# Row sums with a constant matrix as weights, and the norm's factor computed on 128x256

## The chip, the cores and the metric

The kernel runs on one core of one Trainium2 chip. Its time is the device time of one execution in microseconds; times within the trace count from the start of the profiled span. Engines: TensorE (PE, its weight loads PEld), VectorE (DVE), ScalarE (ACT), GpSimd (POOL) and SyncE (SP), which issues most DMAs.

## The reference, cut to what matters

Three transformer blocks run one after the other on a sequence of 256 tokens of width 1024. Block 1 is two mixers, a layer norm, an expert layer with product keys and a second layer norm. Block 2 is two layers of a mixer (nsa, then fox) and a squared-ReLU MLP, with a root-mean-square norm before and after each. Block 3 is mlstm, a gated feed-forward layer, hgrn and a mixture of experts, each behind a norm, and a final norm. What the change touches is the factor of these norms:

```python
def rms_norm(x, g):
    xf = x.astype(jnp.float32)
    y = xf * lax.rsqrt(jnp.mean(xf * xf, axis=-1, keepdims=True) + NORM_EPS)
    return (y * g.astype(jnp.float32)).astype(x.dtype)

def layer_norm(x, g, b):
    ...
    var = jnp.mean(jnp.square(xf - mu), axis=-1, keepdims=True)
    y = (xf - mu) * lax.rsqrt(var + LN_EPS) * g.astype(jnp.float32) + b.astype(jnp.float32)

# in the second block
x = x + rms_norm(m, norm_g[i, 1])
h = rms_norm(x, norm_g[i, 2])
x = x + rms_norm(squared_relu_mlp(h, mlp_w_up[i], mlp_w_down[i]), norm_g[i, 3])
```

## The kernel before

Activations lie transposed in SBUF: the 1024 features are eight tiles of 128 partitions (KT = 8), and the 256 tokens are the columns (T = 256). A norm therefore sums over partitions, which a matmul does, and its factor is one number per token, that is per column, and the same on all partitions.

Weights are streamed from HBM in tiles raw of 128x1024 by SyncE's queue. ScalarE rounds each into hi (L316) and VectorE forms the rest lo (L317), four buffers of each; mm3 (L327 to L329) makes three matmuls out of every product. lin_chunk makes one accumulator mm of 128x512 out of 48 such matmuls; there are two mm buffers.

A norm goes like this. Squares collects the squares of eight tiles of x in two tiles of 128x512: the first is the sum of three pairs, the second holds the last pair. fold (L494) sums each over partitions by add_sum (L359): the data are the weights, the constant column onesD is what moves, and the outcome is 128x2 in PSUM, tokens on partitions. It makes 8 matmul calls, each two passes in the trace. rstd (L371) computes the factor on 128x2: the root on ScalarE (L376), then v, the reciprocal, two products and a last step on VectorE (L377 to L381):

```python
nc.scalar.activation(t, var, AF.Sqrt, bias=self.C(eps))
nc.vector.tensor_scalar(v, var, eps, -0.5, op0=OP.add, op1=OP.mult)
nc.vector.reciprocal(r, t)
nc.vector.tensor_tensor(t, r, r, op=OP.mult)
nc.vector.tensor_tensor(t, t, v, op=OP.mult)
nc.vector.scalar_tensor_tensor(r, t, 1.5, r, op0=OP.add, op1=OP.mult)
```

spread (L388) brings the 128x2 back to 128x256 on all partitions by two matmul calls, four passes, into PSUM (L391):

```python
self.nc.tensor.matmul(ps[:, i * 128:i * 128 + 128], r[:, i:i + 1].to_broadcast([128, 128]),
                      self.C("ident"), start=True, stop=True)
```

Five places of the code use the factor, called at fourteen places of the program. The layer norms (yk, L453) and rms (yk, L415) and the final norm (L2001) read it from PSUM. add_normed (L473) copies it to SBUF first (rsb, L475) and multiplies (yk, L480), four times. inverse (L504) copies both forms, icol of 128x2 and irow of 128x256 (L507, L508), and is called in nsa, in both squared-ReLU MLPs and in fox, where the factor is multiplied into the outcome of a product and not into its input. In the MLP that is hr (L1039), the first reader of an up chunk's accumulator. A fifteenth norm, the router's, uses its factor as 128x2.

No order is written out by hand: a scheduler places the instructions of each engine in one row, by the dependences and its own estimates, so a change of the norm's code also moves what stands around it.

Of the kernel before, what the change touches and what calls it, by code (L numbers as in the profile page):

```python
# [16 lines left out]
AF = mybir.ActivationFunctionType  # L17
OP = mybir.AluOpType
# [4 lines left out]
T = 256  # L23
# [8 lines left out]
ADDS = 4  # L32
LNV = 8
EPS = (1e-6, 1e-5)
BASE = ("warm", "rs_v", "rs_r", "rs_t", "sqk", "yk", "sq2", "icol")

INV_FREQ = np.float32(10000.0) ** (-np.arange(0, 64, 2, dtype=np.float32) / np.float32(64))

# [178 lines left out]
class Core:  # L217
# [61 lines left out]
    def small(self, shape, dt=F32, tag="s", bufs=2):  # L279
        pool = self.base if tag in BASE else self.kept.get(tag, self.sm)  # L280
        return pool.tile([128] + list(shape), dt, tag=tag, bufs=bufs, name=self.name(tag))
# [114 lines left out]

        self.nc.tensor.matmul(ps, self.C("onesD"), x, start=first, stop=last)

    def rstd_rows(self, sums, eps):
        return self.spread(self.ms_ps()[:, :T], self.rstd(sums[:, :2], eps))  # L400

    def squares(self, x):
        s = Squares(self)
# [64 lines left out]
    def add_normed(self, x, src, gm, sq, g=None):  # L468

        nc = self.nc
        r = self.rstd_rows(self.fold(sq), 1e-6)  # L473
        rs = self.small([T], tag="rsb", bufs=1)
        nc.scalar.activation(rs, r, AF.Copy)  # L475
        nxt = Squares(self, None if g is not None else nc.vector)
        parts = (self.big([KT, T], F32R, nm="nhi"), self.big([KT, T], F32R, nm="nlo")) if g is not None else None
        for k in range(KT):
            m = self.small([T], tag="yk", bufs=3)
            nc.vector.scalar_tensor_tensor(m, src(k), gm[:, k:k + 1], rs, op0=OP.mult, op1=OP.mult)  # L480
            eng = nc.vector if k < ADDS else nc.gpsimd
            eng.tensor_tensor(x[:, k], x[:, k], m, op=OP.add)
            if g is not None:
                self.scaled(x, k, g, parts)
            if k % 2:
                nxt.add(x[:, k - 1:k + 1])
        return nxt, parts
# [5 lines left out]

    def fold(self, sq):  # L494

        ps = self.sums()
        n = len(sq.tiles)
        for i, t in enumerate(sq.tiles):
            for f in range(2):
                self.add_sum(ps, 0, t[:, f], i + f == 0, i == n - 1 and f == 1, square=False)  # L500
        return ps

    def inverse(self, sums, eps=1e-6):

        r = self.rstd(sums[:, :2], eps)
        col, row = self.small([2], tag="icol", bufs=1), self.small([T], tag="irow", bufs=1)
        self.nc.vector.tensor_copy(col, r)  # L507
        self.nc.scalar.activation(row, self.spread(self.ms_ps()[:, :T], r), AF.Copy)  # L508
        return col, row

    def accumulate(self, w, hid, ys, first, last, dts=range(8)):

# [519 lines left out]
def squared_relu(c, x, sq, hs, l, g=None):  # L1032
    nc, d = c.nc, c.d
    ps0, inv = [], []

    def evac(ps):
        r = c.small([2, T], tag="hr")
        row = inv[0][1][:, None, :].to_broadcast([128, 2, T])
        nc.vector.scalar_tensor_tensor(r, ps, 0.0, row, op0=OP.max, op1=OP.mult)  # L1039
        s = c.small([2, T], tag="hs")  # L1040
        nc.scalar.activation(s, r, AF.Square)
        h = (c.small([2, T], F32R, tag="hhi"), c.small([2, T], F32R, tag="hlo"))
        c.split(s, h[0], h[1])
        return h

    def hidden(j):
        ps = c.lin_chunk(d[f"up{l}"][j], hs)
        if j == 0:
            inv.append(c.inverse(c.fold(sq)))
        return evac(ps)  # L1050

    ys = c.long_sum(16, hidden, d[f"down{l}"])
    squares = Squares(c, nc.vector)
    for b in range(4):
        squares.add(ys[b])
    return c.add_normed(x, lambda k: ys[k // 2][:, k % 2], c.V(f"ng{l}3"), squares, g)
# [14 lines left out]
def small_tok(c, src, n, xs):  # L1071

    nc = c.nc
    w = c.wsplit(src, KT)
    ps = c.ms_ps()[:n, :T]
    for k in range(KT):
        c.mm3(ps, w[k], (xs[0][:, k], xs[1][:, k]), k == 0, k == KT - 1)
    zt = c.small([T], tag="zt", bufs=1)
    nc.scalar.activation(zt[:n], ps, AF.Copy)
    pt = c.ms_ps()[:, :2 * n].rearrange("p (a b) -> p a b", a=2)  # L1080
    for tt in range(2):
        nc.tensor.transpose(pt[:, tt], zt[:n, tt * 128:tt * 128 + 128], c.C("ident")[:n, :n])
    return pt
# [8 lines left out]
def nsa(c, x, sq, hs):  # L1092
    nc, d = c.nc, c.d
# [7 lines left out]
    kc, vc = kc[:, 0], kc[:, 1]  # L1101
    K2 = c.big([4, 2, T], nm="K2")
    ps = c.lin_chunk(d["nsa_in"][4], hs)
    col, row = c.inverse(c.fold(sq))
    rv = rp.rearrange("p (a t) -> p a t", a=4)
    nc.vector.tensor_tensor(rv, rv, row[:, None, :].to_broadcast([128, 4, T]), op=OP.mult)

# [116 lines left out]
    ps = small_tok(c, d["nsa_g"], 48, hs)  # L1224
# [3 lines left out]
    v = c.big([2, 2, T], nm="nv")  # L1228
    for br in range(2):
        ps = c.tok_chunk(d["nsa_in"][8 + br], hs)  # L1230
# [67 lines left out]
def fox(c, x, sq, hs):  # L1298
    nc, d = c.nc, c.d
    causal = c.C("causal")  # L1300
    k, v = c.big([KT, T], nm="fk"), c.big([2, D], nm="fv")
# [1 line left out]
    pad_heads(c, q)  # L1303
    bf = bcast_row(c, d["rows16"], 0, 16, "bf")
    ps0 = c.lin_chunk(d["fox_in"][0], hs)
    col, row = c.inverse(c.fold(sq))
    row = row[:, None, :].to_broadcast([128, 2, T])
    z, lf = c.small([2, 16], tag="fz", bufs=1), c.small([2, 16], tag="flf", bufs=1)
    ps = small_tok(c, d["fox_f"], 16, hs)
# [3 lines left out]
    ps = c.ms_ps()  # L1313
# [6 lines left out]
    for j in range(4):  # L1320
        ps = c.lin_chunk(d["fox_in"][j], hs) if j else ps0
# [4 lines left out]
    for j in range(4):  # L1326
        ps = c.tok_chunk(d["fox_in"][8 + j], hs)
# [59 lines left out]
def block2(c, x, sq, hs):  # L1387

    with c.phase("nsa", 8):
        sq, hs = nsa(c, x, sq, hs)  # L1390
    with c.phase("mlp0", 8):
        sq, hs = squared_relu(c, x, sq, hs, 0, c.V("ng10"))
    with c.phase("fox", 8):
        sq, hs = fox(c, x, sq, hs)
    with c.phase("mlp1", 8):
        return squared_relu(c, x, sq, hs, 1)[0]
# [368 lines left out]
class Router:  # L1765
# [34 lines left out]

    def finish(self, sq):
        c, nc = self.c, self.c.nc
        r = c.rstd(c.fold(sq)[:, :2], 1e-6)
        lt = c.small([T], tag="lt", bufs=1)
        nc.scalar.activation(lt[:8], self.lg, AF.Copy)
        pt = c.ac_ps()[:, :16].rearrange("p (a e) -> p a e", a=2)
        lg = c.small([2, 8], tag="lg", bufs=1)
        for tt in range(2):
            nc.tensor.transpose(pt[:, tt], lt[:8, tt * 128:tt * 128 + 128], c.C("ident")[:8, :8])
        for tt in range(2):  # L1810
            nc.vector.scalar_tensor_tensor(lg[:, tt], pt[:, tt], r[:, tt:tt + 1], self.bias, op0=OP.mult, op1=OP.add)
        found = places(c, lg)
        parts = (c.big([2, D], F32R, nm="xhi"), c.big([2, D], F32R, nm="xlo"))
        for tt in range(2):
            for a in range(0, D, 512):
                w = slice(a, a + 512)
                t = self.xt[:, tt, w]
                nc.vector.scalar_tensor_tensor(t, t, r[:, tt:tt + 1], self.row[:, w], op0=OP.mult, op1=OP.add)
                c.split(t, parts[0][:, tt, w], parts[1][:, tt, w])
        return parts, found  # L1820
# [216 lines left out]
```

## Time and profile before

| | |
|---|---|
| median of 3 runs | 2934.7 us |
| lowest and highest run | 2927.17, 2935.34 us |
| the profiled execution | 2925.78 us |
| its span | 2924.1 us |
| mean granted TensorE clock | 0.975 of full speed |
| TensorE matmul busy | 2818.6 us, 96% |
| VectorE busy | 2063.4 us, 71% |
| ScalarE busy | 1543.8 us, 53% |
| GpSimd busy | 156.8 us, 5% |

A timeline row gives the start in us, the length in us, engine, line, operation, what is written and read, and how many instructions are merged into it; brackets hold the idle time of the engine before it and what ended it.

### The profile page before, as it was taken

How to read it: one execution, taken by the hardware profiler on the slowest of the kernel's cores; microseconds unless marked ns; L12 is line 12 of the kernel's file. 1: busy time of each engine (PE TensorE's matmuls, PEld its weight loads, DVE VectorE, ACT ScalarE, POOL GpSimd, SP SyncE). 2: the span in 40 equal slices, each digit the busy share in tenths (PEclk: the TensorE clock that was granted, in tenths of full speed). 3: DMA queues.
4: the chain of work that ended last, by engine and by line, in shares of the span. 5: the costliest groups of instructions: out<-in, count | busy, mean ns of one | idle time of the engine just before them, and what ended most of it. 6: DMA issues, size and time to landing. Idle time of an engine off the chain costs nothing. (4 is left out here: it accounts for less than half of the span.)

```text
span 2924.1 us, 51291 instructions
## 1 busy us (share of the span) xinstructions
PE 2818.6 (96%) x20880; PEld 2666.6 (91%) x20880; DVE 2063.4 (71%) x3757; ACT 1543.8 (53%) x2196; POOL 156.8 (5%) x137
## 2 busy tenths in 40 slices
PE   8999999899999999999999999989999998999998
PEld 8998989899999999887999989989899997888886
DVE  6655979777777785667655565565655696899997
ACT  5454317544444444457444464445544645777775
POOL 0000000000000000210001000001000170000000
PEclk9999999999999999899999999989999999999998
DMA  7543346888888786341454415534255432789885
GB/s 277 209 155 136 134 144 231 288 302 297 299 302 298 283 300 230 123 176 47 145 185 146 173 59 188 182 108 159 102 188 188 141 129 87 295 331 336 324 331 211
DMA packets 118901, 602.23 MB, mean 206 GB/s; under 512 B 10752, under 2 KB 46080, under 8 KB 49664
## 3 DMA queue, kind: packets, MB, share of 16 engines
q1 hardware_dynamic: 78480, 557.96, 53.1%
q10 hardware_dynamic: 40176, 40.91, 4.4%
q8 instruction: 166, 2.72, 0.4%
q14 instruction: 79, 0.65, 0.1%
HBM read 579.43 MB, written 19.39 MB: 205 GB/s over the span
## 5 line engine op out<-in xcount | busy, mean ns | idle before, releaser
L317 DVE TENSOR_TENSOR lo<-raw,hi 128x1024 fp32r<-128x1024 f32 x915 | 1126.2, 1244 | 590.4 <-ACT hi L316 586.9
L316 ACT ACTIVATE hi<-raw 128x1024 fp32r<-128x1024 f32 x915 | 960.9, 1057 | 926.5 <-PE mm L328 507.5
L327 PE MATMUL mm<-nhi,hi 128*128 128x256 f32 x1312 | 378.6, 290 | 10.2 <-ACT nhi L491 6.8
L328 PE MATMUL mm<-nlo,hi 128*128 128x256 f32 x1312 | 378.9, 289 | 0.5 <-DVE nlo L492 0.5
L329 PE MATMUL mm<-nhi,lo 128*128 128x256 f32 x1312 | 376.7, 287 | 0.0
L329 PE MATMUL mm<-lhi,lo 128*128 128x256 f32 x1024 | 295.1, 288 | 7.7 <-DVE lo L317 7.7
L327 PE MATMUL mm<-lhi,hi 128*128 128x256 f32 x1024 | 294.9, 289 | 5.1 <-ACT r L933 2.8
L328 PE MATMUL mm<-llo,hi 128*128 128x256 f32 x1024 | 295.6, 289 | 0.0
L328 PE MATMUL ac<-r,hi 128*128 128x256 f32 x1024 | 288.2, 282 | 0.0
L329 PE MATMUL ac<-r,lo 128*128 128x256 f32 x1024 | 288.0, 281 | 0.0
L327 PE MATMUL ac<-r,hi 128*128 128x256 f32 x1024 | 287.7, 281 | 0.0
L327 PEld LDWEIGHTS mm<-nhi,hi 128*128 128x128 f32 x1312 | 257.5, 197 | 12.2 <-ACT nhi L491 7.5
L328 PEld LDWEIGHTS mm<-nlo,hi 128*128 128x128 f32 x1312 | 257.7, 197 | 2.5 <-DVE nlo L492 1.7
L329 PEld LDWEIGHTS mm<-nhi,lo 128*128 128x128 f32 x1312 | 257.7, 197 | 0.1
L329 PEld LDWEIGHTS mm<-lhi,lo 128*128 128x128 f32 x1024 | 201.0, 196 | 9.0 <-DVE lo L317 8.1
L327 PEld LDWEIGHTS mm<-lhi,hi 128*128 128x128 f32 x1024 | 201.2, 197 | 6.9 <-ACT r L933 3.0
L328 PEld LDWEIGHTS mm<-llo,hi 128*128 128x128 f32 x1024 | 200.9, 196 | 1.1 <-issue 0.7
L328 PE MATMUL ac<-hlo,hi 128*128 128x256 f32 x688 | 193.0, 281 | 0.0
L328 PEld LDWEIGHTS ac<-r,hi 128*128 128x128 f32 x1024 | 192.9, 188 | 0.0
L327 PE MATMUL ac<-hhi,hi 128*128 128x256 f32 x688 | 192.8, 280 | 0.0
L329 PEld LDWEIGHTS ac<-r,lo 128*128 128x128 f32 x1024 | 192.7, 188 | 0.0
L327 PEld LDWEIGHTS ac<-r,hi 128*128 128x128 f32 x1024 | 192.7, 188 | 0.0
(590 smaller groups left out, 6288.9 us busy)
## 6 DMA issues: line engine op xcount, KB each, us to landing
raw<-in_moe_gu SPq DMA_DIRECT2D x88, 1024.0 KB, 5.1
raw<-in_peer_u SPq DMA_DIRECT2D x64, 1024.0 KB, 5.0
raw<-in_peer_v SPq DMA_DIRECT2D x64, 1024.0 KB, 5.5
raw<-in_ada SPq DMA_DIRECT2D x48, 1024.0 KB, 7.2
raw<-in_moe_d SPq DMA_DIRECT2D x40, 1024.0 KB, 5.5
raw<-in_up SPq DMA_DIRECT2D x32, 1024.0 KB, 4.9
raw<-in_down SPq DMA_DIRECT2D x32, 1024.0 KB, 4.9
raw<-in_ffn_gu SPq DMA_DIRECT2D x22, 1024.0 KB, 4.9
```

The source lines that it names most:

```text
L316: nc.scalar.activation(hi, raw[:, a:a + m], AF.Copy)
L317: nc.vector.tensor_tensor(lo, raw[:, a:a + m], hi, op=OP.subtract)
L327: mm(ps, w[0], x[0], start=start, stop=False, **k)
L328: mm(ps, w[0], x[1], start=False, stop=False, **k)
L329: mm(ps, w[1], x[0], start=False, stop=stop, **k)
```

## The change

fold sums with the constant matrix onesD (128x128) as weights, and the squares move, 256 columns a call (rows_add, which the layer norm's mean used already): 4 calls instead of 8, and the outcome is 128x256 in PSUM, the same on all partitions. The factor is computed on this 128x256 by the same six steps and stands in SBUF at the end. The spread, the copy rsb and the copy irow are gone. Where tokens are needed on partitions (icol in nsa and fox), column takes two columns out of irow with two matmuls of one column and a VectorE copy. The router keeps the old way under the name fold_cols. The scratch memory for dynamic DMA is halved.

```diff
+    def rstd_rows(self, sums, eps, out=None):
+        nc = self.nc
+        v, r, t = (self.small([T], tag=g, bufs=1) for g in ("rr_v", "rr_r", "rr_t"))
+        m = sums[:, :T]
+        nc.scalar.activation(t, m, AF.Sqrt, bias=self.C(eps))
+        nc.vector.tensor_scalar(v, m, eps, -0.5, op0=OP.add, op1=OP.mult)
+        nc.vector.reciprocal(r, t)
+        nc.vector.tensor_tensor(t, r, r, op=OP.mult)
+        nc.vector.tensor_tensor(t, t, v, op=OP.mult)
+        out = r if out is None else out
+        nc.vector.scalar_tensor_tensor(out, t, 1.5, r, op0=OP.add, op1=OP.mult)
+        return out
...
-    def rstd_rows(self, sums, eps):
-        return self.spread(self.ms_ps()[:, :T], self.rstd(sums[:, :2], eps))
...
-        r = self.rstd_rows(self.fold(sq), 1e-6)
-        rs = self.small([T], tag="rsb", bufs=1)
-        nc.scalar.activation(rs, r, AF.Copy)
+        rs = self.rstd_rows(self.fold(sq), 1e-6)
...
     def fold(self, sq):
+        ps = self.ms_ps()
+        n = len(sq.tiles)
+        for i, t in enumerate(sq.tiles):
+            for f in range(2):
+                self.rows_add(ps[:, :T], t[:, f], i + f == 0, i == n - 1 and f == 1)
+        return ps
...
     def inverse(self, sums, eps=1e-6):
-        r = self.rstd(sums[:, :2], eps)
-        col, row = self.small([2], tag="icol", bufs=1), self.small([T], tag="irow", bufs=1)
-        self.nc.vector.tensor_copy(col, r)
-        self.nc.scalar.activation(row, self.spread(self.ms_ps()[:, :T], r), AF.Copy)
-        return col, row
+        return self.rstd_rows(sums, eps, out=self.small([T], tag="irow", bufs=1))
+
+    def column(self, row):
+        ps = self.ms_ps()[:, :2]
+        for i in range(2):
+            self.nc.tensor.matmul(ps[:, i:i + 1], row[:, i * 128:i * 128 + 128], self.C("ident")[:, :1], start=True, stop=True)
+        col = self.small([2], tag="icol", bufs=1)
+        self.nc.vector.tensor_copy(col, ps)
+        return col
...
-    col, row = c.inverse(c.fold(sq))
+    row = c.inverse(c.fold(sq))
+    col = c.column(row)
...
-        r = c.rstd(c.fold(sq)[:, :2], 1e-6)
+        r = c.rstd(c.fold_cols(sq)[:, :2], 1e-6)
...
-    nc = bacc.Bacc("TRN2", target_bir_lowering=False, num_devices=1, dynamic_dma_scratch_size=8192)
+    nc = bacc.Bacc("TRN2", target_bir_lowering=False, num_devices=1, dynamic_dma_scratch_size=4096)
```

The change also moves instructions. On VectorE, at the norm in front of hgrn, the row before is this (rs_ are the small tiles of the factor, ms the spread factor, yk the normed input):

```order
L377 TENSOR_SCALAR rs_v_24364<-ms_24354 128x2 [waits Activation_49]
L378 RECIPROCAL rs_r_24365<-rs_t_24366 128x2
L379 TENSOR_TENSOR rs_t_24366<-rs_r_24365 128x2 [waits DVE_49]
L380 TENSOR_TENSOR rs_t_24366<-rs_t_24366,rs_v_24364 128x2 [waits DVE_49]
L381 SCALAR_TENSOR_TENSOR rs_r_24365<-rs_t_24366,rs_r_24365 128x2 [waits DVE_49]
L317 TENSOR_TENSOR lo_24478<-raw_24471,hi_24477 128x1024 [waits Activation_49]
L415 SCALAR_TENSOR_TENSOR yk_24377<-x,mg_24352,ms_24363 128x256 [waits PE_49]
```

and now, with rr_ for the factor's tiles:

```order
L405 TENSOR_SCALAR rr_v_24265<-ms_24260 128x256 [waits Activation_49]
L406 RECIPROCAL rr_r_24266<-rr_t_24267 128x256
L317 TENSOR_TENSOR lo_24377<-raw_24370,hi_24376 128x1024 [waits Activation_49]
L407 TENSOR_TENSOR rr_t_24267<-rr_r_24266 128x256 [waits DVE_49]
L408 TENSOR_TENSOR rr_t_24267<-rr_t_24267,rr_v_24265 128x256 [waits DVE_49]
L410 SCALAR_TENSOR_TENSOR rr_r_24266<-rr_t_24267,rr_r_24266 128x256 [waits DVE_49]
L426 SCALAR_TENSOR_TENSOR yk_24276<-x,mg_24258,rr_r_24266 128x256 [waits DVE_49]
```

The split lo, which stood behind the last step and ahead of yk, has moved between the reciprocal and the first product.

On VectorE, in the first squared-ReLU MLP, the row before runs from the second norm's small steps to the first hr:

```order
L378 RECIPROCAL rs_r_14935<-rs_t_14936 128x2
L379 TENSOR_TENSOR rs_t_14936<-rs_r_14935 128x2 [waits DVE_49]
L380 TENSOR_TENSOR rs_t_14936<-rs_t_14936,rs_v_14934 128x2 [waits DVE_49]
L381 SCALAR_TENSOR_TENSOR rs_r_14935<-rs_t_14936,rs_r_14935 128x2 [waits DVE_49]
L507 COPY icol_14943<-rs_r_14935 128x2 [waits DVE_49]
L317 TENSOR_TENSOR lo_15032<-raw_15025,hi_15031 128x1024 [waits PE_49,Activation_49]
L1039 SCALAR_TENSOR_TENSOR hr_14950<-mm_14876,irow_14944 128x512 [waits Activation_49]
```

and now:

```order
L317 TENSOR_TENSOR lo_14994<-raw_14987,hi_14993 128x1024 [waits PE_49,Activation_49]
L405 TENSOR_SCALAR rr_v_14903<-ms_14897 128x256 [waits Activation_49]
L406 RECIPROCAL rr_r_14904<-rr_t_14905 128x256 [waits DVE_49]
L407 TENSOR_TENSOR rr_t_14905<-rr_r_14904 128x256 [waits DVE_49]
L317 TENSOR_TENSOR lo_15048<-raw_15045,hi_15047 128x1024 [waits DMAHW5_49,PE_49,Activation_49]
L408 TENSOR_TENSOR rr_t_14905<-rr_t_14905,rr_v_14903 128x256 [waits DVE_49]
L410 SCALAR_TENSOR_TENSOR irow_14902<-rr_t_14905,rr_r_14904 128x256 [waits DVE_49]
L1062 SCALAR_TENSOR_TENSOR hr_14912<-mm_14848,irow_14902 128x512 [waits DVE_49]
```

One split has moved ahead of v, and one stands between the two products. The second MLP has the same rows.

On TensorE, in fox, the spread stood between the last matmuls of the first chunk and the narrow projection of 16 columns:

```order
L327 MATMUL mm_17004<-nhi_16927,hi_17000 128x256
L328 MATMUL mm_17004<-nlo_16928,hi_17000 128x256
L329 MATMUL mm_17004<-nhi_16927,lo_17001 128x256
L391 MATMUL ms_17074<-cst,rs_r_17063 128x128 [waits DVE_49,PE_49]
L391 MATMUL ms_17074<-cst,rs_r_17063 128x128
L327 MATMUL ms_17086<-nhi_16927,hi_17082 16x256 [waits PE_49]
```

and now the column stands there, behind the second chunk:

```order
L327 MATMUL mm_17089<-nhi_16880,hi_17085 128x256
L328 MATMUL mm_17089<-nlo_16881,hi_17085 128x256
L329 MATMUL mm_17089<-nhi_16880,lo_17086 128x256
L529 MATMUL ms_17021<-cst,irow_17011 128x1 [waits DVE_49,PE_49]
L529 MATMUL ms_17021<-cst,irow_17011 128x1
L327 MATMUL ms_17034<-nhi_16880,hi_17030 16x256
```

What TensorE waits for there has changed from the 128x2 factor to irow.

## Rows read from the trace of the kernel before

**Rows 1.** The page's busy time by engine: us, share, instructions.

```profile
PE 2818.6 (96%) x20880; PEld 2666.6 (91%) x20880; DVE 2063.4 (71%) x3757; ACT 1543.8 (53%) x2196; POOL 156.8 (5%) x137
```

**Rows 2.** TensorE's waits: us in total, times, the longest.

```profile
PE ms L391 <- DVE rs_r L381: 13.3, 10, 2.2
```

**Rows 3.** Timeline of the first layer norm.

```profile
273.36 3.17 PE L368 MATMUL ms<-cst,sq 128*128 128x1 f32 x16 [3.98 <-DVE sq L565]
...
276.56 0.26 ACT L376 ACTIVATE rs_t<-ms,cst 128x2 f32<-128x2 f32 x1 [2.13 <-PE ms L368]
...
276.94 0.15 DVE L378 RECIPROCAL rs_r<-rs_t 128x2 f32<-128x2 f32 x1
...
277.52 0.16 DVE L381 SCALAR_TENSOR_TENSOR rs_r<-rs_t,rs_r 128x2 f32<-128x2 f32 x1
...
277.73 1.22 PE L391 MATMUL ms<-cst,rs_r 128*128 128x128 f32 x4 [1.21 <-DVE rs_r L381]
278.99 0.75 DVE L453 TENSOR_TENSOR yk<-x,ms 128x256 f32<-128x256 f32 x2 [1.32 <-PE ms L391]
```

**Rows 4.** Timeline, TensorE: a mean in layer norm two, a fold.

```profile
1195.82 3.62 PE L397 MATMUL ms<-x,cst 128*128 128x256 f32 x16
...
1929.70 2.00 PE L368 MATMUL ms<-cst,sq 128*128 128x1 f32 x16
```

**Rows 5.** VectorE by line and shape: count, busy us, mean ns of one.

```profile
L453 DVE TENSOR_TENSOR yk<-x,ms 128x256 f32<-128x256 f32 x16 | 6.0, 414 | 2.6 <-PE ms L391 2.6
...
L378 DVE RECIPROCAL rs_r<-rs_t 128x2 f32<-128x2 f32 x15 | 2.3, 155 | 0.0
...
L378 DVE RECIPROCAL rs_r<-rs_t 128x8 f32<-128x8 f32 x4 | 0.8, 194 | 0.0
...
L1193 DVE RECIPROCAL cst<-cst 128x16 f32<-128x16 f32 x2 | 0.5, 253 | 0.1
```

**Rows 6.** Timeline, add_normed after nsa.

```profile
1387.19 0.26 ACT L376 ACTIVATE rs_t<-ms,cst 128x2 f32<-128x2 f32 x1 [0.87 <-PE ms L368]
...
1389.10 0.38 ACT L475 ACTIVATE rsb<-ms 128x256 f32<-128x256 f32 x1 [1.66 <-PE ms L391]
1389.52 0.88 DVE L480 SCALAR_TENSOR_TENSOR yk<-mix,vecs,rsb 128x256 f32<-128x256 f32 x2 [1.22 <-ACT rsb L475]
```

**Rows 7.** Timeline, add_normed after fox.

```profile
1734.30 0.26 ACT L376 ACTIVATE rs_t<-ms,cst 128x2 f32<-128x2 f32 x1 [0.87 <-PE ms L368]
...
1737.14 0.88 DVE L480 SCALAR_TENSOR_TENSOR yk<-mix,vecs,rsb 128x256 f32<-128x256 f32 x2 [1.73 <-ACT rsb L475]
```

**Rows 8.** Timeline, add_normed at the end of the second MLP.

```profile
1931.85 1.23 DVE L317 TENSOR_TENSOR lo<-raw,hi 128x1024 fp32r<-128x1024 f32 x1 [0.27 <-ACT hi L316]
...
1932.99 0.15 DVE L377 TENSOR_SCALAR rs_v<-ms 128x2 f32<-128x2 f32 x1
...
1935.54 0.88 DVE L480 SCALAR_TENSOR_TENSOR yk<-ac,vecs,rsb 128x256 f32<-128x256 f32 x2 [1.73 <-ACT rsb L475]
```

**Rows 9.** Timeline, the norm in front of hgrn.

```profile
2288.38 0.26 ACT L376 ACTIVATE rs_t<-ms,cst 128x2 f32<-128x2 f32 x1 [3.27 <-PE ms L368]
...
2289.61 1.23 DVE L317 TENSOR_TENSOR lo<-raw,hi 128x1024 fp32r<-128x1024 f32 x1
...
2290.86 1.26 DVE L415 SCALAR_TENSOR_TENSOR yk<-x,mg,ms 128x256 f32<-128x256 f32 x3
```

**Rows 10.** Timeline, inverse in the first MLP.

```profile
1407.14 0.39 ACT L508 ACTIVATE irow<-ms 128x256 f32<-128x256 f32 x1
```

**Rows 11.** Timeline, the spread in nsa.

```profile
1226.97 0.60 PE L391 MATMUL ms<-cst,rs_r 128*128 128x128 f32 x4
```

**Rows 12.** Stretches: length, busy by engine, granted clock; full clock, then twelve low stretches.

```profile
286.00:290.00 4.00, 4.00 (x35) 4.00 (x34) 2.32 (x5) 1.93 (x3) 0.00 (x0) 1.00 0.00 0
...
273.80:284.10 10.30, 7.95 (x35) 7.39 (x35) 5.82 (x21) 3.77 (x10) 0.00 (x0) 0.50 0.00 1
...
sum 117.40, PE 78.36 PEld 72.73 DVE 70.53 ACT 42.45 POOL 20.18; mean PE 6.53 PEld 6.06 DVE 5.88 ACT 3.54 POOL 1.68
```

More of the change, by code (lines that the diff above doesn't have):

```diff
@@ L34 @@
 EPS = (1e-6, 1e-5)
-BASE = ("warm", "rs_v", "rs_r", "rs_t", "sqk", "yk", "sq2", "icol")
+BASE = ("warm", "rs_v", "rs_r", "rs_t", "rr_v", "rr_r", "rr_t", "sqk", "yk", "sq2", "icol")
 INV_FREQ = np.float32(10000.0) ** (-np.arange(0, 64, 2, dtype=np.float32) / np.float32(64))
@@ L494, in fold, with fold_cols @@
     def fold(self, sq):
+        ps = self.ms_ps()
[4 more added lines that the diff above has]
+        return ps
+    def fold_cols(self, sq):
         ps = self.sums()
@@ L1037, in evac @@
         r = c.small([2, T], tag="hr")
-        row = inv[0][1][:, None, :].to_broadcast([128, 2, T])
+        row = inv[0][:, None, :].to_broadcast([128, 2, T])
         nc.vector.scalar_tensor_tensor(r, ps, 0.0, row, op0=OP.max, op1=OP.mult)
@@ L1305, in fox @@
     ps0 = c.lin_chunk(d["fox_in"][0], hs)
-    col, row = c.inverse(c.fold(sq))
+    row = c.inverse(c.fold(sq))
+    col = c.column(row)
     row = row[:, None, :].to_broadcast([128, 2, T])
```

## The prediction

> **What bounds the kernel now.** I began with the busy shares. TensorE is busy 2818.6 us of the 2924.1 us span [rows 1], so a change counts through the 105 us in which TensorE stands still, or through the length of TensorE's own work. The view of waits then says which part of those 105 us belongs to the code that changes: ten times the spread waits for the last VectorE step of the factor, 13.3 us in total, at most 2.2 us each [rows 2]. The timeline of the first layer norm shows one such wait whole [rows 3]: sixteen passes of the fold end at 276.53, ScalarE's root starts 0.03 us later, VectorE's steps on 128x2 follow some 0.2 us apart and end at 277.68, the spread occupies TensorE from 277.73 to 278.95, and the first product with the factor (yk) starts at 278.99. So from the end of the sums to yk, 2.46 us pass in which nothing else is ready, and whatever the change does to these 2.46 us goes straight to the end. The same holds at ten of the fourteen changed places: two layer norms, the four add_normed, three rms and the final norm. At the four calls of inverse (nsa, both squared-ReLU MLPs, fox) the spread stands behind other matmuls, and TensorE keeps working during the chain.
>
> **What is removed and added, step by step.** *The fold* falls from sixteen passes of one column to eight passes of 256. Sixteen old passes took 2.00 us at full clock; sixteen passes of the new kind (the layer norm's mean, L397) took 3.62 us [rows 4], so eight cost 1.81 us. The gain of 0.2 us lies on the path only where the fold does, and at half clock the old passes took 3.17 us [rows 3], where eight new ones, at twice 0.226 us, would take 3.6. I take nothing for it at the ten waiting places, with bounds of -0.2 and +0.4 us each.
>
> *The root* goes from 128x2 to 128x256. It took 0.26 us; a ScalarE copy of 128x256 out of PSUM took 0.38 [rows 3, 6]. With the bias I take 0.47, +0.2.
>
> *The tail v, square, times v, last step* goes from starts 0.2 us apart to the pace of 128x256. Two yk in a row took 0.75 us, one 0.414 us [rows 3, 5], so v holds the pipe 0.36 us before the next may start; a dependent step costs its length and the 0.04 us seen between the 128x2 steps (reciprocal to last step, three starts in 0.58 us at 0.15 each). So 0.36 + 0.46 + 0.46 + 0.51.
>
> *The reciprocal* decides. The trace has it at three sizes: 155 ns for 2 columns, 194 for 8, 253 for 16 [rows 5]. That is 6.5 and 7.4 ns for each further column, 7.0 over the whole, where a product or a copy grows by about 1 ns (0.16 us at 2 columns, 0.414 at 256 [rows 3, 5]). Carried on to 256 columns: 155 + 254 x 6.5 to 7.4 = 1.8 to 2.03 us; I take 1.90. The other end is a reciprocal that streams like its neighbours, 0.42 us. I choose the upper end because it is the same instruction on the same type and its three rows lie on a line.
>
> The Trainium skill bears on this one: "VectorE: DVE Perf Modes", section "First, the fixed hardware budget", says that the reciprocal is an iterative divide with a repeat count of 8 in the pipe that takes one element a cycle otherwise. The three rows agree in kind (7.0 ns a column against 1). By the page's count, 8 cycles at 0.96 GHz, an estimate is 2.1 us for 256 columns, and the sum below would be some 2 to 3 us higher.
>
> The new chain from the end of the sums to the consumer is then 0.03 + 0.47 + 0.04 + 0.36 + 1.94 + 0.46 + 0.46 + 0.51 = **4.27 us**. It replaces the old small steps, the spread and, in add_normed, the copy rsb.
>
> **The ten places.** In the layer norms and the final norm 2.46 becomes 4.27: +1.8 each, 5.4. In add_normed after nsa the root starts at 1387.19 and yk at 1389.52, 2.36 us with the 0.03 ahead of the root, at full clock and with the copy of 0.38 [rows 6]: +1.9; the end of the first MLP has the same steps: together 3.8. After fox the spread is at half clock, so more goes away: 2.87 us [rows 7] become 4.27, +1.4. At the end of the second MLP a 1.23 us split of weights (lo) holds v back until 1932.99 anyway, the longer root hides under it, and 2.55 us from v to yk [rows 8] become 3.73: +1.2. The rms of hgrn takes 2.51 us from the sums to yk [rows 9], and those of mlstm and of the feed-forward have the same steps: +1.7 or 1.8 each, 5.2. In hgrn one thing more: the split lo that ran beside the spread, from 2289.61 [rows 9], stands between the reciprocal and the square in the new order, since there is no spread left to run beside: its 1.23 us come onto the path, +1.2. Sum of the ten: 5.4 + 3.8 + 1.4 + 1.2 + 5.2 + 1.2 = **18.2 us**.
>
> What is late next: after each chain yk, the split and the first matmul follow as before, and all three wait on the factor alone, so no other wait takes up the delay.
>
> **The four inverse places.** TensorE loses four spreads of 0.60 us [rows 11] and 0.2 us of fold each, and gets two columns (two passes of 128x1 and their weight loads, 0.25 us a pass by the fold's 2.00 us for sixteen, at most 0.5 us with the switch): -2.4 - 0.8 + 1.0 = -2.2 us. Before, the chain was hidden: in the first MLP irow is copied from 1407.14 to 1407.53 [rows 10] and TensorE doesn't wait for it. Now TensorE has the second up chunk, 48 matmuls, left after the last fold pass, 48 x 0.114 = 5.5 us by 35 in 4.00 us at full clock [rows 12]. Then it needs hr, since the third chunk wants the accumulator of the first. In VectorE's new order the chain is cut by splits: one before v and one between the two products. Root and v, 0.9; reciprocal 1.94; 0.46 + 1.23 + 0.46 + 0.51; with up to 1.2 us for the first split: 6.7 us, and hr 0.69: 7.4 us. TensorE waits 7.4 - 5.5, about 2 us, in both MLPs. In fox the column's matmul, which waits for irow at once, follows straight behind that chunk, with one split in VectorE's chain: +1.4. Queued behind it are the narrow f projection and the next chunk, which need neither. In nsa 58 matmuls, 6.6 us, stand ahead of the column: 0, with up to +2 if both splits come late. Together +5.4 - 2.2 = **+3.2 us**. The bounds here are -2.2 (all covered) and +8.
>
> The scratch size for dynamic DMA changes no queue that moves data here, and the router keeps the old fold and 128x2 chain: 0.
>
> **The sum.** 18.2 + 3.2 = +21.4 us on the profiled execution of 2925.78 us, so 2947.2. That execution lay 0.3% under the median of the runs, 2934.7; carried to it: **2956 us**.
>
> **The rivals.**
>
> *A, the reciprocal streams.* Against it speak the three sizes. It would take 0.42 us, 1.48 less: the ten places give 3.4, the inverse places about -1: 2934.7 + 2.4 = 2937. That would be no measurable change.
>
> *B, faster: the clock stays up.* In twelve stretches around these places, 117.4 us, the granted clock is 0.50 on average, that is 1.2 instead of 2.4 GHz, and TensorE is busy in 78.4 us of them [rows 12]; at full clock the same work would take 39.2 us less. The new fold feeds 256 columns a pass where the old one fed one. If that kept the clock at 2.4 GHz in these stretches, the time would be 2956 - 39 = 2917. It decides from 22 us on, 56% of all that is there. Against it: in the first layer norm TensorE stood still for 4 us before the fold began [rows 3], on squares that the change doesn't make sooner, and the wait after the fold gets longer, not shorter.
>
> *C, worse: the inverse places lose their cover altogether and the low clock lasts as much longer as the waits do.* A low clock that lasts 1.8 us longer once TensorE runs again costs half of that in lost work: ten places by up to 0.9 us, 9; with the upper bound of the inverse places, +5: 2970.
>
> *D, covered in part.* If ScalarE and VectorE put off splits that in the old order followed the factor, the restart may find more weights ready; a third of the ten places' cost would be 6 us: 2950, in the forecast's own range.
>
> **How the numbers follow.** Forecast (with D) 0.75, range 2942 to 2964; A 0.10; B 0.05; C 0.10. The range for 8 in 10 leaves out B, and the outer halves of A and C: 2937 to 2970. A measurement of this kernel tells 0.3%, 8.8 us, from no change, so slower begins at 2943.5. Of the forecast's 0.75, 0.70 lies above that; with C 0.80. A and the forecast's low end make 0.15 for the same, B 0.05 for faster.
>
> **What would show it.** In the changed kernel's trace, RECIPROCAL on 128x256 should read 1.8 to 2.0 us (A: 0.4); from the end of the fold to yk 4.2 to 4.4 us at the first layer norm and the final norm; a split between the reciprocal and the square at hgrn; TensorE idle about 2 us for hr's accumulator in both MLPs, and on the column in fox. The sum of the stretches at clock 0.50 stays near 117 us; B needs it under 60. The forecast is wrong if these chains are as long as said and TensorE's idle time all the same grows by less than 10 us.

## The result, and the profile after

The changed kernel takes 2951.8 us (median of 4 runs, 2950.1 to 2955.6) against 2933.7 us before (4 runs, 2927.2 to 2935.3). That is 18.2 us more by the medians. The ratio of the runs is put at 1.0072, with a 95% interval of 1.0054 to 1.0089; it is not the quotient of the two medians (1.0062), and its interval stands for 16 to 26 us, so the times alone can't tell 18 us from the 21.4 that were forecast. The forecast was 2956 us. The profiled execution took 2950.14 us, its span 2948.4.

The busy time by engine on the page of the changed kernel answers to [rows 1]:

```profile
PE 2807.5 (95%) x20720; PEld 2647.1 (90%) x20720; DVE 2097.9 (71%) x3755; ACT 1544.2 (52%) x2188; POOL 158.2 (5%) x137
```

TensorE has 11.1 us less to do and stands still for 140.9 us instead of 105.5. So TensorE's work did shrink, for the most part by the fourteen spreads (14.4 us), and three times as much idle time came in its place. Most of it stands in the factor's chain: from the root to yk at the ten waiting places TensorE is idle for 41.7 us instead of 15.0, and 11.1 us of the old chains were the spreads' own work. Here is the timeline of the first layer norm after, against [rows 3]; weight loads are left out:

```profile
277.19 3.78 PE L397 MATMUL ms<-sq,cst 128*128 128x256 f32 x8 [3.98 <-DVE sq L588]
...
281.01 0.47 ACT L404 ACTIVATE rr_t<-ms,cst 128x256 f32<-128x256 f32 x1 [2.75 <-PE ms L397]
281.51 0.42 DVE L405 TENSOR_SCALAR rr_v<-ms 128x256 f32<-128x256 f32 x1 [4.05 <-ACT rr_t L404]
281.85 1.74 DVE L406 RECIPROCAL rr_r<-rr_t 128x256 f32<-128x256 f32 x1
283.63 0.42 DVE L407 TENSOR_TENSOR rr_t<-rr_r 128x256 f32<-128x256 f32 x1
284.09 0.42 DVE L408 TENSOR_TENSOR rr_t<-rr_t,rr_v 128x256 f32<-128x256 f32 x1
284.55 0.42 DVE L410 SCALAR_TENSOR_TENSOR rr_r<-rr_t,rr_r 128x256 f32<-128x256 f32 x1
285.00 0.76 DVE L464 TENSOR_TENSOR yk<-x,rr_r 128x256 f32<-128x256 f32 x2
...
286.12 0.80 PE L327 MATMUL mm<-lhi,hi 128*128 128x256 f32 x2 [5.15 <-ACT lhi L465]
```

From the root's start to yk it is 3.99 us where it was 2.43. TensorE's one wait of 5.15 us replaces two, the 1.21 us before the spread [rows 3] and the 1.15 us behind it in this row of before, since no spread stands between them any more:

```profile
280.10 0.79 PE L327 MATMUL mm<-lhi,hi 128*128 128x256 f32 x2 [1.15 <-ACT lhi L454]
```

The reciprocal is the longest step by far. By line and shape (count, busy us, mean ns of one), VectorE shows, against [rows 5]:

```profile
L406 DVE RECIPROCAL rr_r<-rr_t 128x256 f32<-128x256 f32 x14 | 24.4, 1743 | 0.0
L408 DVE TENSOR_TENSOR rr_t<-rr_t,rr_v 128x256 f32<-128x256 f32 x14 | 5.9, 424 | 0.4
L405 DVE TENSOR_SCALAR rr_v<-ms 128x256 f32<-128x256 f32 x14 | 5.9, 423 | 24.0 <-ACT rr_t L404 24.0
L407 DVE TENSOR_TENSOR rr_t<-rr_r 128x256 f32<-128x256 f32 x14 | 5.9, 422 | 0.4
L410 DVE SCALAR_TENSOR_TENSOR rr_r<-rr_t,rr_r 128x256 f32<-128x256 f32 x10 | 4.3, 426 | 0.3
```

The fold costs about the same, as TensorE's rows by line and shape show, the first of after and the second of before (240 passes there, 16 of them the router's, 1.8 us, so the fourteen folds went from 36.6 to 38.4 us):

```profile
L397 PE MATMUL ms<-sq,cst 128*128 128x256 f32 x112 | 38.4, 478 | 36.6 <-DVE sq L588 22.2 <-POOL sq L588 5.3 <-DVEq L1893 5.3
```

```profile
L368 PE MATMUL ms<-cst,sq 128*128 128x1 f32 x240 | 38.4, 283 | 28.9 <-DVE sq L565 18.2 <-DVEq L1868 5.1 <-ACT sq L557 3.7
```

At hgrn the split stands where the order had put it, inside the chain, and yk starts 4.96 us after the root instead of 2.48 [rows 9]:

```profile
2308.66 0.47 ACT L404 ACTIVATE rr_t<-ms,cst 128x256 f32<-128x256 f32 x1 [2.58 <-PE ms L397]
...
2309.51 1.74 DVE L406 RECIPROCAL rr_r<-rr_t 128x256 f32<-128x256 f32 x1
2311.17 1.16 DVE L317 TENSOR_TENSOR lo<-raw,hi 128x1024 fp32r<-128x1024 f32 x1
2312.25 0.41 DVE L407 TENSOR_TENSOR rr_t<-rr_r 128x256 f32<-128x256 f32 x1
...
2313.62 1.27 DVE L426 SCALAR_TENSOR_TENSOR yk<-x,mg,rr_r 128x256 f32<-128x256 f32 x3
```

TensorE's waits (us in total, times, the longest) have changed; against [rows 2], the wait on rs_r is gone:

```profile
PE ms L397 <- DVE sq L588: 22.2, 4, 11.5
PE mm L327 <- ACT nhi L500: 18.0, 4, 5.9
PE mm L327 <- ACT nhi L430: 16.4, 3, 6.1
PE mm L327 <- ACT lhi L465: 10.3, 2, 5.2
...
PE ms L397 <- POOL sq L588: 5.3, 4, 2.0
...
PE mm L327 <- DVE hr L1062: 2.6, 2, 1.3
...
PE ms L529 <- DVE irow L410: 1.0, 1, 1.0
```

The three waits on ScalarE (ACT) are the restart behind eight of the ten waiting places, 44.3 of their 44.7 us. Behind the ninth, the end of the second MLP, the restart is the fold of the next norm, whose 11.5 us were 7.3 before; behind the final norm TensorE has nothing left to do. The last two rows, on hr and irow, are new: both MLPs and fox. The wait of 2.0 us for GpSimd's sum of squares is the first MLP's (0.8 before); fox has one of 1.9 us.

The whole span difference of the two executions, 24.3 us, can be laid out by the starts of the root and of yk at the ten places:

| stretch | before, us | after, us | difference |
|---|---|---|---|
| start to the root of layer norm one | 276.56 | 281.01 | +4.45 |
| ten chains, root to yk | 26.1 | 41.7 | +15.6 |
| around nsa's inverse (yk to the next waiting root) | 177.89 | 176.94 | -0.95 |
| around the first MLP's | 196.50 | 198.27 | +1.77 |
| around fox's | 145.95 | 146.93 | +0.98 |
| around the second MLP's | 194.60 | 196.35 | +1.75 |
| layer norm one to two | 927.88 | 926.43 | -1.45 |
| mlstm | 141.03 | 143.08 | +2.05 |
| all else | | | +0.15 |

Chains and inverse places make 19.2 us, near the 18.2 of the medians. Two long stretches behind norms are what they were: from the feed-forward's norm to hgrn's 196.3 us in both, from hgrn's to the final one 624.1 in both. The start is scatter: from 38 to 47 us both kernels run the same code, and this execution had the low clock there; the one of before first fell under full clock at 273.8 us. The stretches below (length, busy by engine, granted clock third from the right) are of after and of before:

```profile
38.00:42.00 4.00, 4.00 (x17) 2.94 (x16) 2.83 (x6) 2.42 (x6) 0.00 (x0) 0.77 0.47 131
42.00:46.00 4.00, 4.00 (x17) 3.35 (x16) 2.31 (x8) 1.96 (x3) 0.00 (x0) 0.50 0.65 250
```

```profile
38.00:42.00 4.00, 4.00 (x23) 3.05 (x22) 2.46 (x6) 2.95 (x5) 0.00 (x0) 1.00 0.52 172
```

mlstm has the same kind of scatter: 140.6 to 145.7 us over the profiled executions of the ten kernels, long in those with more time at the low clock there.

### The profile page after: what moved, and what is told of

It is laid out like the page before. It is cut to its first block, busy times and chain, and to the rows that moved or that the text cites. A ratio compares the mean times of both kernels' runs of the same rounds, so it can differ in the third digit from the quotient of the medians.

```text
span 2948.4 us, 50950 instructions
## 1 busy us (share of the span) xinstructions
PE 2807.5 (95%) x20720; PEld 2647.1 (90%) x20720; DVE 2097.9 (71%) x3755; ACT 1544.2 (52%) x2188; POOL 158.2 (5%) x137
## 5 line engine op out<-in xcount | busy, mean ns | idle before, releaser
L329 PE MATMUL ac<-hhi,lo 128*128 128x256 f32 x688 | 192.4, 280 | 0.0
```

The lines of the kernel that those rows point to most:

```text
L329: mm(ps, w[1], x[0], start=False, stop=stop, **k)
```

## The experiments

Two theories stood against each other. L: the chain's length goes to the end. O: the moved instructions and the new fold cost the time, and the chain's length is covered. Ratios are to the kernel before on the same chip. Its median is 2927.8 to 2933.7 us, depending on the chip and the set of runs, so a difference between two experiments of different sets is good to a few microseconds only.

**The reciprocal taken out.**

```diff
-        nc.scalar.activation(t, m, AF.Sqrt, bias=self.C(eps))
+        nc.scalar.activation(r, m, AF.Abs_reciprocal_sqrt, bias=self.C(eps))
         nc.vector.tensor_scalar(v, m, eps, -0.5, op0=OP.add, op1=OP.mult)
-        nc.vector.reciprocal(r, t)
```

The function that loads ScalarE's table ahead of time (L386) is changed with it, here and in the other kernels below that use this function.

> The changed kernel with the reciprocal taken out of the chain: ScalarE computes one over the root in the place of the root, and v, the square, the product and the last step refine it as before. The row sums, the 128x256 layout and the missing spread stay. Theory L: the chain falls from 4.0 to 2.2 us, 1.78 x 10 = 17.8 less, and the waits on hr and on the column (3.6 us) go: 2930 to 2932, at or a little below the kernel before. Theory O: 2948 or more, since nothing but the reciprocal is gone.

Measured: 2929.7 us (10 runs), ratio 0.9989, 0.9979 to 0.9999. The whole loss is gone and nothing but the reciprocal was taken out of the factor. The order moved with it: in both MLPs the split between the two products no longer stands in the chain. The new fold, the split in hgrn's chain (3.23 us from root to yk) and the halved scratch memory all remain in this kernel without a loss, so O falls. The timeline of its first layer norm shows the same chain without that step, 2.21 us from root to yk:

```profile
277.18 0.47 ACT L404 ACTIVATE rr_r<-ms,cst 128x256 f32<-128x256 f32 x1 [2.57 <-PE ms L397]
277.68 0.42 DVE L405 TENSOR_SCALAR rr_v<-ms 128x256 f32<-128x256 f32 x1 [3.88 <-ACT rr_r L404]
278.03 0.41 DVE L406 TENSOR_TENSOR rr_t<-rr_r 128x256 f32<-128x256 f32 x1
278.47 0.42 DVE L407 TENSOR_TENSOR rr_t<-rr_t,rr_v 128x256 f32<-128x256 f32 x1
278.93 0.42 DVE L409 SCALAR_TENSOR_TENSOR rr_r<-rr_t,rr_r 128x256 f32<-128x256 f32 x1
279.39 0.76 DVE L463 TENSOR_TENSOR yk<-x,rr_r 128x256 f32<-128x256 f32 x2
```

ScalarE's function takes as long as the root did (0.47 us), so it is no gain of its own.

**The reciprocal twice.**

```diff
         nc.vector.reciprocal(r, t)
+        nc.vector.reciprocal(r, t)
```

> The changed kernel with the 128x256 reciprocal issued twice in a row at all fourteen places. Theory L (the length of the chain sums-to-consumer goes to the end one to one at the ten waiting places, and shows beyond the cover at the inverse places): +1.74 us x 10 = 17.4, and 1.7 us more at the two MLPs and fox, which already wait, 5; nsa 0 to 1. Together +22 to +24 on 2951.8, so about 2974. Theory O (the moved instructions and the new fold cost the time, and the chain lies beside other work): within 4 us of 2952.

Measured: 2983.3 us (4 runs), ratio 1.0168, 1.0144 to 1.0192. That is 31.5 us over the changed kernel by the medians, 28 by the ratios, where L said 22 to 24: the direction and the ten chains are as said (1.79 us each, 17.9), but in its trace the stretches around the inverse places took 17.9 more and not 5. Its waits of TensorE there:

```profile
PE mm L327 <- DVE hr L1063: 8.1, 2, 4.1
PE ms L530 <- DVE irow L411: 3.7, 1, 3.7
```

In each MLP the wait grew from 1.3 to 4.1 us, since one more split (1.16 us, at 1425.92) came to stand in the longer chain, and after the wait the clock fell. The stretches of the first MLP; in the first matmuls after the wait TensorE does 10 or 11 in 2 us instead of 19:

```profile
1427.00:1429.00 2.00, 0.00 (x0) 0.00 (x0) 1.97 (x5) 0.14 (x1) 0.00 (x0) 1.00 0.01 4
1429.00:1431.00 2.00, 0.79 (x4) 0.82 (x5) 1.63 (x3) 0.87 (x2) 0.00 (x0) 0.67 0.73 180
1431.00:1433.00 2.00, 2.00 (x10) 1.87 (x10) 1.08 (x2) 1.54 (x3) 0.00 (x0) 0.50 0.82 344
1433.00:1435.00 2.00, 2.00 (x11) 2.00 (x11) 0.30 (x1) 0.00 (x0) 0.00 (x0) 0.50 0.00 0
1435.00:1437.00 2.00, 2.00 (x13) 2.00 (x13) 0.00 (x0) 0.24 (x1) 0.00 (x0) 0.63 0.03 8
1437.00:1439.00 2.00, 2.00 (x19) 2.00 (x18) 1.15 (x1) 0.82 (x1) 0.00 (x0) 1.00 0.00 0
```

The second MLP shows the same after its wait (0.50 from 1796 to 1800 us). The changed kernel's wait of 1.3 us at the same place leaves the clock at 1.00. So the waits of 4.1 us cost more than their length here: they are 2.8 us longer than in the changed kernel, and the two stretches are longer by 5.6 and 6.9 us.

**The ten places as before.**

```diff
-        rs = self.rstd_rows(self.fold(sq), 1e-6)
+        r = self.spread(self.ms_ps()[:, :T], self.rstd(self.fold_cols(sq)[:, :2], 1e-6))
+        rs = self.small([T], tag="rsb", bufs=1)
+        nc.scalar.activation(rs, r, AF.Copy)
...
```

> The changed kernel with the old way (one-column fold, 128x2 chain, spread, and the copy rsb in add_normed) put back at the ten waiting places; the four inverse places keep the new way. Theory L: the ten places' 15.6 us (read from the two traces) go away, the inverse places' 3 to 4 us stay: 2936 to 2938. Theory O: the row folds and the order at the inverse places hold most of the cost, so 2944 or more.

Measured: 2940.5 us (10 runs), ratio 1.0032, 1.0020 to 1.0043, so 8.2 us over the kernel before. Between the theories, nearer to L: 10 us of the 18 went with the ten chains, where L expected 15.6. In its trace the four stretches around the inverse places are 4.0, 1.6, 0.8 and 1.7 us longer than before, 8.2 in all, and nsa's is the one that differs from the changed kernel's.

**The inverse places as before.**

```diff
-        return self.rstd_rows(sums, eps, out=self.small([T], tag="irow", bufs=1))
+        r = self.rstd(sums[:, :2], eps)
+        col, row = self.small([2], tag="icol", bufs=1), self.small([T], tag="irow", bufs=1)
+        self.nc.vector.tensor_copy(col, r)
+        self.nc.scalar.activation(row, self.spread(self.ms_ps()[:, :T], r), AF.Copy)
+        return col, row
...
```

The four calls sum with fold_cols again.

> The changed kernel with the old way put back at the four inverse places only (nsa, both MLPs, fox); the ten waiting places keep the new way. Theory L: 3 to 4 us less than 2951.8, about 2948. Theory O (inverse places and their order hold the cost): 2940 or less.

Measured: 2953.0 us (4 runs), ratio 1.0064, 1.0040 to 1.0087: against the changed kernel 1.2 us more by the medians and 2 less by the ratios. No gain is shown, but the interval can't rule out the 4 us less that L expected; the 12 less of O lie outside it. The page shows where the idle time went that this edit did save:

```profile
PE 2816.1 (95%) x20760; PEld 2657.5 (90%) x20760; DVE 2090.7 (71%) x3757; ACT 1545.4 (52%) x2192; POOL 158.0 (5%) x137
```

Against the changed kernel TensorE stands still 5.3 us less (span 2951.7) and is busy 8.6 us longer. The four spreads and the old folds can be some 3 of those, and the clock goes far enough for the rest: added up from stretches of 1 us over the whole span, TensorE was busy for 103.3 us at the low clock here and 87.5 in the changed kernel, and half of the 15.8 is 7.9 us. Fox and the second MLP have 13.4 and 12.4 us of low clock here instead of 8.2 and 6.8. That the edit brought this about is not shown; one execution can't tell it from scatter.

**The ten places and nsa as before.**

```diff
-    row = c.inverse(c.fold(sq))
-    col = c.column(row)
+    col, row = c.inverse_cols(sq)
```

on top of the ten (inverse_cols is the old inverse; nsa alone).

> The kernel with the ten waiting places as before, and nsa's inverse as before too; the two MLPs and fox keep the new way. It asks why the kernel with the ten places alone undone stood 8 us above the kernel before and not 4: in its trace TensorE waits 3.2 us for irow at nsa's column, which the fully changed kernel doesn't. If that wait is the surplus (theory N): 4 us less than 2940.5, about 2936.5. If the surplus is spread over all places or lies in the execution's own scatter (theory S): 2939 to 2942.

Measured: 2939.1 us (5 runs, 2933.9 to 2941.7), ratio 1.0036, 1.0022 to 1.0050. Not less than with the ten alone. The expectation had also put the wait of 3.2 us in the wrong place: it is fox's column, and it stands in this trace too. What lengthened nsa's stretch with the ten alone is another wait, for a product on GpSimd (rraw), and a low clock behind it, as the waits and a stretch of that trace show; this kernel's trace, the changed kernel's and that of the kernel before don't have this wait (two reciprocals have one of 2.4 us):

```profile
PE ac L1165 <- POOL rraw L1032: 2.6, 1, 2.6
```

```profile
1246.00:1248.00 2.00, 2.00 (x7) 0.80 (x4) 1.99 (x4) 0.00 (x0) 0.00 (x0) 0.50 0.04 8
```

Its profiled execution, the lowest of its runs, has nsa's stretch 5.7 us shorter, but its runs don't show that as a gain. So the price of the new inverse with the old ten is 8 us by the medians, 11 with nsa as before, and 3.6 us by the stretches of the changed kernel. Part of the difference is seen: the wait on fox's column is 3.2 us with the old ten and 1.0 in the changed kernel. The rest stays open.

**One step in the changed layout.**

```diff
+        r = self.small([T], tag="rr_r", bufs=1) if out is None else out
+        nc.scalar.activation(r, sums[:, :T], AF.Abs_reciprocal_sqrt, bias=self.C(eps))
+        return r
```

in the place of the six steps.

> The changed layout with ScalarE's one over the root alone as the factor; all VectorE steps of the factor are left out, so the factor isn't refined. Theory L: the chain falls from 4.00 us to 0.52, and the waits on hr and on the column go: 10 x 3.48 + 4 = 39 less than 2951.8, about 2913, if the low clock returns nothing; with part of it given back as the low clock then covers more work, 2913 to 2921. Theory O: no lower than 2929.

Measured: 2914.5 us (4 runs), ratio 0.9934, 0.9908 to 0.9961: 37 us under the changed kernel and 16 under the kernel before. The timeline of its first layer norm:

```profile
281.10 0.47 ACT L403 ACTIVATE rr_r<-ms,cst 128x256 f32<-128x256 f32 x1 [2.75 <-PE ms L397]
281.61 0.76 DVE L457 TENSOR_TENSOR yk<-x,rr_r 128x256 f32<-128x256 f32 x2 [4.05 <-ACT rr_r L403]
```

0.51 us from root to yk. The factor has the accuracy of ScalarE's function alone here; whoever needs the refinement has the kernel without the reciprocal.

**One step in the old layout.**

```diff
-        return self.spread(self.ms_ps()[:, :T], self.rstd(sums[:, :2], eps))
+        return self.spread(self.ms_ps()[:, :T], self.rstd1(sums[:, :2], eps))
```

rstd1 is ScalarE's one step on 128x2, and inverse uses it too.

> The kernel before (one-column fold, 128x2, spread) with the six steps replaced by ScalarE's one step on 128x2, not refined. Theory L: the chain falls from 2.43 to about 1.6 us (root 0.26, spread 1.22, the gaps; 0.4 more with the copy rsb), ten times 0.95 is 9 to 10 less than the kernel before, about 2923, and so above the same step in the changed layout. If the layout made no difference, both would stand within 3 us of each other.

Measured: 2924.4 us (10 runs, 2915.7 to 2931.9), ratio 0.9975, 0.9959 to 0.9991, as L said. Its first layer norm needs 1.58 us from root to yk, most of it the spread at low clock:

```profile
278.29 0.26 ACT L386 ACTIVATE rs_r<-ms,cst 128x2 f32<-128x2 f32 x1 [2.53 <-PE ms L368]
278.61 1.22 PE L396 MATMUL ms<-cst,rs_r 128*128 128x128 f32 x4 [0.35 <-ACT rs_r L386]
279.87 0.75 DVE L458 TENSOR_TENSOR yk<-x,ms 128x256 f32<-128x256 f32 x2 [4.91 <-PE ms L396]
```

So the changed layout is the better one by some 10 us when the factor is one step, and the worse one by 18 when it is six with a reciprocal among them.

**One VectorE step less.**

```diff
-        nc.scalar.activation(t, m, AF.Sqrt, bias=self.C(eps))
-        nc.vector.tensor_scalar(v, m, eps, -0.5, op0=OP.add, op1=OP.mult)
-        nc.vector.reciprocal(r, t)
+        nc.scalar.activation(r, m, AF.Abs_reciprocal_sqrt, bias=self.C(eps))
+        nc.scalar.activation(h, r, AF.Copy, scale=-0.5)
         nc.vector.tensor_tensor(t, r, r, op=OP.mult)
-        nc.vector.tensor_tensor(t, t, v, op=OP.mult)
+        nc.vector.scalar_tensor_tensor(t, m, eps, t, op0=OP.add, op1=OP.mult)
...
-        nc.vector.scalar_tensor_tensor(out, t, 1.5, r, op0=OP.add, op1=OP.mult)
+        nc.vector.scalar_tensor_tensor(out, t, -3.0, h, op0=OP.add, op1=OP.mult)
```

> The changed layout without the reciprocal and with one VectorE step less in the chain: ScalarE makes one over the root and, beside VectorE, minus half of it; VectorE squares, multiplies with the variance and finishes. Theory L: the chain falls from 2.21 us (measured without the reciprocal) to 1.9, ten times 0.3 is 3 less than 2929.7, about 2927. Theory O: no change from 2929.7.

Measured: 2928.8 us (10 runs), ratio 0.9991, 0.9979 to 1.0002. The chain did fall from 2.21 to 1.95 us, but 2.6 us over ten places is within what these runs scatter, and the ratio is that of the kernel without the reciprocal (0.9989): inconclusive in the time.

## Why the prediction was right

The mechanism and the place were right: the ten waiting places carry the loss, the reciprocal is its largest part, and nothing took the delay up. TensorE's idle time grew by 35.4 us, far from the 10 us under which the forecast called itself wrong. Point by point, predicted and read from the trace:

| term | predicted, us | read, us |
|---|---|---|
| reciprocal on 128x256 | 1.90 (1.8 to 2.03) | 1.74 |
| root to yk, layer norms and final | 4.24 | 3.99 to 4.00 |
| added at both layer norms and the final norm | 5.4 | 4.7 |
| nsa's output, end of the first MLP | 3.8 | 3.3 |
| fox's output | 1.4 | 1.2 |
| end of the second MLP | 1.2 | 0.9 |
| three rms | 5.2 | 4.5 |
| the split at hgrn | 1.2 | 1.0 |
| sum of the ten | 18.2 | 15.6 |
| inverse places | 3.2 | 3.6 |

In the ten places the term that was mis-sized is the reciprocal: its 1.743 us is 6.25 ns a column, under the 6.5 to 7.4 that the three small sizes gave, so the lowest slope was the best one and the wide step from 16 to 256 columns the risk. Times ten that is 1.6 of the 2.6 us between 18.2 and 15.6; the rest is the last step, 0.45 us up to yk and not 0.51, v's pace, 0.34 and not 0.36, and the split at hgrn, 1.0 and not 1.2. The Trainium skill ("VectorE: DVE Perf Modes", "First, the fixed hardware budget") has the reciprocal as an iterative divide with a repeat count of 8; read as 8 cycles a column at the page's 0.96 GHz, this gives an estimate of 2.1 us. The measurement, 1.74, is below it, and in kind the row agrees: 6.25 ns a column, where the products grow by about 1.

At the inverse places the sum came out near, and its parts in part: hr's wait was 1.3 us in each MLP instead of 2 and the column's in fox 1.0 instead of 1.4, while TensorE also waited 2.0 us, and not 0.8, for the sum of squares on GpSimd in the first MLP, and 1.9 us in fox, which the prediction didn't have. nsa came out shorter than before, not equal. That the sum is near is luck in part: over the four stretches TensorE's idle time grew by 8.1 us (15.6 to 23.7) where 5.4 was forecast, and its work fell by 4.6 where 2.2 was, and in this execution the low clock lasted 29.8 us of them instead of 41.3. The waits for GpSimd are not the new inverse's either: with the old inverse they are 0.7 us in the first MLP and 1.9 and 2.0 in fox and the second MLP. That the old inverse gave nothing back in its experiment says that the sum of 3.6 us isn't known to better than a few microseconds.

Rival A, the streaming reciprocal, is out by its row. Rival B is out too: added up from stretches of 1 us over the whole span, the low clock lasts 144.8 us before and 143.5 after. C's second half didn't come: the low clock did not grow with the waits; TensorE's work in it fell from 96.9 to 87.5 us, as more of the low time passes while it waits. One reciprocal more brought both halves: the stretches around the inverse places 17.9 us longer, and the low clock 169.8 us. D isn't seen: the chains are the full 4.0 us at every place where nothing else stands in them, the first matmul of layer norm one starts 1.12 us after yk where it was 1.11, and the stretches behind the norms of the feed-forward and hgrn are as long as before.

## What to carry to other kernels

A VectorE step was paid here by its columns, though all 128 partitions held the same numbers, so before a small chain is widened in order to save a transfer, price every step of it at the new width, and the reciprocal apart from the rest: it grew from 0.16 to 1.74 us where the products grew from 0.16 to 0.42. If TensorE waits for the chain, only the chain's length counts: of the spreads' 14.4 us, 11.1 stood inside the ten chains and are part of their old length, not a saving beside it. Taking the slow step out brought the same layout from 18 us slower back to the time of the kernel before (2929.7 us), and one step in the place of the six, without the refinement, to 16 us faster. A chain that hides behind other work has room only up to its cover; past it, waits of 4.1 us in the MLPs were followed by a lower clock, and waits of 1.3 us were not.

## What the runs showed of the hardware

The second layer norm's fold ran at full clock in the changed kernel, eight passes in 1.99 us, where the first layer norm's eight took 3.78 at the low clock, after nearly equal waits of 3.8 and 4.0 us. The clock fell only at the end of the chain behind it. In the kernel with the inverse places as before, whose norm has the same code, the second layer norm's fold took 3.78 us. So the same code meets either clock, depending on the execution:

```profile
1209.40 1.99 PE L397 MATMUL ms<-sq,cst 128*128 128x256 f32 x8 [3.83 <-DVE sq L588]
```

```profile
1210.00:1214.00 4.00, 1.39 (x7) 0.84 (x5) 2.06 (x2) 0.95 (x3) 0.00 (x0) 1.00 0.00 0
1214.00:1218.00 4.00, 1.46 (x5) 1.21 (x6) 3.86 (x12) 1.68 (x4) 0.00 (x0) 0.54 0.00 0
1218.00:1222.00 4.00, 4.00 (x24) 4.00 (x24) 4.00 (x10) 2.71 (x5) 1.86 (x1) 0.61 0.00 0
```

This is where the 1.45 us between the layer norms came from (the old fold had taken 3.57 us there, at the low clock), and with the start and mlstm it is why one profiled execution pins down a chain to 0.01 us but the whole to no better than some 5.
